# A third arm for experts of up to 64 rows, plain fp32 last half-pieces, and expert weights stored piece by piece

## The chip, the cores and the metric

The kernel runs on one core of one Trainium2 chip. The metric is the device time of one execution in microseconds. Before the change, three runs took 2416.90, 2423.72 and 2423.22 us (median 2423.22); the execution that the profiler recorded took 2418.95 us.

## The reference

One block of a diffusion transformer on 2048 rows of 1024 fp32 numbers. A first part (modulated RMS norm, a spatial gating unit, a bidirectional gated linear attention, an output projection) gives h; then comes a mixture of experts with a two-level router, and a final RMS norm:

```python
hn2 = modulate(rmsnorm(h, g_norm2), sh2, sc2)
# router: the best of 8 groups, then the best 2 of its 8 experts; gate = p_top * softmax(l_top)
# for each expert e, on the rows that chose it:
hblk = silu(xblk @ w1[e]) * (xblk @ w3[e])     # 1024 -> 512
yb   = (hblk @ w2[e]) * gate                   # 512 -> 1024, summed back to the rows
h = h + g2 * y
return rmsnorm(h, g_final)
```

There are 64 experts of three 512 x 1024 matrices (6 MB each in fp32) and 2048 x 2 = 4096 choices, 64 rows to an expert on average. With the reference's inputs, 41 experts get 64 rows or fewer, 16 get 65 to 128, and 7 get 129 to 220; the first of these 7 is number 8, the last number 39, and from number 40 on 21 of 24 have 64 or fewer.

## The kernel before

The first part (lines 111 to 842) and the router (lines 845 to 1150) come first. The change touches the expert stage, lines 1153 to 1390.

*Weights.* An expert has 12 pieces of 128 partitions x 1024 columns (512 KB): 8 for w1 and w3 side by side ("up"), 4 for w2 ("down"). `seq` (line 596) orders them: up of e+1, then down of e. `wload` (line 604) puts one DMA per piece on SyncE's queue, into the oldest of NR = 28 buffers. In DRAM, w_e is laid out by expert, partition, piece, so each partition's 4 KB of a piece lie 48 KB from the next partition's.

*fp32 in three passes.* Both operands of a product are split in a high part rounded to fp32r (ScalarE, a copy) and the remainder (VectorE, a subtraction), and TensorE runs high x high, high x low and low x high: three fp32r matmuls instead of one in plain fp32. `split_w` (line 79) does it for a half-piece of 512 columns, into a ring of R = 8 pairs wh and wl (line 1227); `need` (line 1232) keeps the splits LA = 4 half-pieces ahead of the matmuls in program order. The rows' side is split by `xprep` (line 1192: TensorE transposes the gathered rows, ScalarE and VectorE split them into xhe and xle) and by `hsplit` (line 1205, into hhe and hle).

*Order.* The schedule is written by hand: each engine executes its instructions in program order. One turn of the loop over e (line 1372) does `up(e + 1)`, counts and loads, then `down(e)`. Inside `block` (line 1256) a table `at` hangs other work on half-piece numbers: `hsplit` at half-piece 4 of up; `xprep` of the expert after next at half-piece 4 of down; the transposes of the GLU's result at half-piece 6. `glu` (line 1210) is a Silu on ScalarE and a product on VectorE, `yevac` (line 1214) scales the down result on VectorE, `scat` adds it to the output rows by an indirect DMA on GpSimd's queue.

*Arms.* How many rows an expert has is known on the device only. `count` (line 1277) reads nblk, the number of blocks of 128 rows, into a register of every engine, and up and down each have two arms under `tc.If`: `two` (above 128 rows; each split half-piece serves two blocks) and `one`. `both` (line 1239) emits the two with the same ring positions. `more` (line 1268) gathers the second block's rows, and `rest` (line 1290) handles blocks beyond the second.

Of the kernel before, what the change touches and what calls it, by code (L numbers as in the profile page):

```python
# [23 lines left out]
G, NE, EG, F = 8, 64, 8, 512  # L24
KF = F // P
# [5 lines left out]
def kernel(ctx: ExitStack, tc: tile.TileContext, a: dict, out: bass.AP):  # L31
    nc = tc.nc
    vec, act, pool, pe, sp = nc.vector, nc.scalar, nc.gpsimd, nc.tensor, nc.sync

    ctx.enter_context(tc.manual_schedule())
    const = ctx.enter_context(tc.tile_pool(name="const", bufs=1))
# [75 lines left out]
    wk = es.enter_context(tc.tile_pool(name="p1a", bufs=1))  # L112
# [112 lines left out]
    KG, PV, KZ, VV, LA, PB, PR, KDt, KE = ({} for _ in range(9))  # L225
# [182 lines left out]
    for half in range(2):  # L408
        for j in range(2):
            pm[j] = pt("mm", [P, 512], "pm")  # L410
        for k in range(KD):
            for j in range(2):
                pe.matmul(pm[j][0:2], sig[:, k], mtile[half * KD + k][:, j * 512:(j + 1) * 512],
                          start=k == 0, stop=k == KD - 1)
# [184 lines left out]
            seq += [(e + 1, k) for k in range(KD)]  # L599
        seq += [(e, KD + k) for k in range(KF)]  # L600
    W, WT = {}, []
    NW, NR = 25, 28

    def wload(n, eng=sp):

        for m in range(len(W), min(n, len(seq))):
            if m < NR:
                WT.append((wa if m < 14 else wb if m < NW else wk).tile([P, D], F32, name=f"we{m}", tag="w" if m < NW else f"we{m}"))
            e, k = seq[m]
            W[e, k] = WT[m % NR]  # L610
            eng.dma_start(out=W[e, k], in_=a["w_e"][e, :, k * D:(k + 1) * D])

    es = ExitStack()
    wk = es.enter_context(tc.tile_pool(name="p1c", bufs=1))
# [173 lines left out]
    for it in range(NT):  # L788
        ti = T - it
        n = ti - 1  # L790
# [59 lines left out]
    wk = es.enter_context(tc.tile_pool(name="p1d", bufs=1))  # L850
# [302 lines left out]
    nblk = const.tile([1, NE], I32, name="nblk")  # L1153
# [20 lines left out]
    four = lambda t: t.rearrange("p (c n) -> p c n", c=4)  # L1174
# [2 lines left out]
    ci_ = wk.tile([1, NE], I32, name="ci_")  # L1177
    vec.tensor_scalar(ci_, pc[0:1], float(P - 1), None, op0=OP.add)
    vec.tensor_scalar(nblk, ci_, 7, None, op0=OP.logical_shift_right)
    most = wk.tile([1, 1], I32, name="most")  # L1180
    vec.tensor_reduce(most, nblk, axis=mybir.AxisListType.X, op=OP.max)
    BOUND = "a count of at most S rows over blocks of P"

    xhl = [wk.tile([P, KD, P], F32R, name=n) for n in ("xhe", "xle")]
    hx = [wk.tile([P, KF, P], F32R, name=n) for n in ("hhe", "hle")]
    hx2 = [wk.tile([P, KF, P], F32R, name=n) for n in ("hh2", "hl2")]
    sh = wk.tile([P, F], F32, name="she")
    sh2 = [wk.tile([P, F], F32, name=f"sh2{i}") for i in range(2)]
    y1 = wk.tile([P, D], F32, name="y1")
# [2 lines left out]
    def xprep(x, hl, tp):  # L1192
        xh, xl = hl
        for c in range(KD):
            pe.transpose(four(tp[c // 4])[:, c % 4], x[:, c * P:(c + 1) * P], ident)  # L1195
        for q in range(2):
            qs = slice(4 * q, 4 * q + 4)
            act.activation(xh[:, qs], four(tp[q]), AF.Copy)
            vec.tensor_tensor(xl[:, qs], four(tp[q]), xh[:, qs].bitcast(F32), op=OP.subtract)

    def htr(sh, th):
        for i in range(KF):
# [2 lines left out]
    def hsplit(th, hx):  # L1205
        hh, hl = hx
        act.activation(hh, four(th), AF.Copy)
        vec.tensor_tensor(hl, four(th), hh.bitcast(F32), op=OP.subtract)

    def glu(pa, sh):  # L1210
# [18 lines left out]
    hpos = {v: p for p, v in enumerate(hseq)}  # L1229
    nsp = 0  # L1230

    def need(p):
        nonlocal nsp
        while nsp <= min(p, len(hseq) - 1):
            e, k, i = hseq[nsp]
            split_w(W[e, k][:, i * 512:(i + 1) * 512], *ring[nsp % R])
            nsp += 1

    def both(two, one):

        nonlocal nsp
        n0 = nsp
        two()
        n1, nsp = nsp, n0
        yield
        one()
        assert nsp == n1

    def mms(o, hl, k, i, nk, ring_):
        mm3(o, hl[0][:, k], hl[1][:, k], *ring_, k == 0, k == nk - 1)  # L1250
# [2 lines left out]

        return [t.rearrange("p (k n) -> p k n", k=KD) for t in (xgr[e % 3], xqr[e % 2])]

    def block(base, n, outs, hls, at):

        for q in range(n + (LAG if len(outs) > 1 else 0)):
            if q < n:
                need(base + q + LA)  # L1260
                if q in at:
                    at[q]()
            for j, (o, hl) in enumerate(zip(outs, hls)):
                p = q - j * LAG
                if 0 <= p < n:
                    mms(o[p % 2], hl, p // 2, p % 2, n // 2, ring[(base + p) % R])

    def more(e):

        n = nc.values_load(nblk[0:1, e:e + 1], engines=[mybir.EngineType.Pool], min_val=0, max_val=S // P,  # L1270
                           skip_runtime_bounds_check_because=BOUND)
        with tc.If(n > 1, preferred_fallthrough_block=False):
            gath(xq[e % 2], col(idx, NE + e))

    NB_ = {}

    def count(e):
        return nc.values_load(nblk[0:1, e:e + 1], min_val=0, max_val=S // P, skip_runtime_bounds_check_because=BOUND)

    def again(e, ks, outs, hl):  # L1280

        wh, wl = ring[nsp % R]
        raw = y2[:, F:]
        for k in range(ks[0], ks[1]):
            for i in range(2):
                pool.dma_start(out=raw, in_=a["w_e"][e, :, k * D + i * 512:k * D + (i + 1) * 512])
                split_w(raw, wh, wl)
                mms(outs[i], hl, k - ks[0], i, ks[1] - ks[0], (wh, wl))

    def rest():  # L1290

        x, hl = xq[0], rows2(0)
        n = nc.values_load(most, min_val=0, max_val=S // P, skip_runtime_bounds_check_because=BOUND)
        with tc.If(n > 2, preferred_fallthrough_block=False):
            for e in range(NE):
                n = count(e)
                with tc.If(n > 2, preferred_fallthrough_block=False):
                    with tc.For_i(2, n, 1) as i:
                        tb2 = wk.tile([P, 2], F32, name="tb2")
                        pool.dma_start(out=tb2, in_=tabD[bass.ds(i * P + e * S, P)])  # L1300
                        ix2 = wk.tile([P, 1], I32, name="ix2")
                        pool.tensor_copy(ix2, tb2[:, 0:1])
                        gath(x, ix2)
                        xprep(x, hl, TP)
                        again(e, (0, KD), PA, hl)
                        glu(PA, y2[:, 0:F])
                        htr(y2[:, 0:F], TH[1])
                        hsplit(TH[1], hx2)
                        again(e, (KD, KD + KF), PA, hx2)
                        yevac(PA, tb2[:, 1:2], y2)  # L1310
                        scat(y2, ix2)

    def up(e):

        at = {4: lambda: hsplit(TH[0], hx)} if e else {}
        base = hpos[e, 0, 0]

        def two():
            xprep(xq[e % 2], rows2(e), PY)
            block(base, 2 * KD, (PA, TP), (xhl, rows2(e)), at)  # L1320
            glu(PA, sh)
            glu(TP, sh2[e % 2])

        def one():
            block(base, 2 * KD, (PA,), (xhl,), at)
            glu(PA, sh)

        g = both(two, one)
        with tc.If(NB_[e] > 1, preferred_fallthrough_block=False) as f:
            next(g)  # L1330
        with f.Else():
            next(g, None)

    def down(e):

        base = hpos[e, KD, 0]
        at = {}
        if e + 2 < NE:
            at[4] = lambda: xprep(xg[(e + 2) % 3], xhl, TP)
        if e + 1 < NE:  # L1340
            at[6] = lambda: htr(sh, TH[0])

        def two():
            htr(sh2[e % 2], TH[1])
            hsplit(TH[1], hx2)
            block(base, 2 * KF, (PY, PA), (hx, hx2), at)
            yevac(PA, col(gate, NE + e), y2)
            scat(y2, col(idx, NE + e))

        def one():  # L1350
            block(base, 2 * KF, (PY,), (hx,), at)

        g = both(two, one)
        with tc.If(NB_[e] > 1, preferred_fallthrough_block=False) as f:
            next(g)
        with f.Else():
            next(g, None)
        yevac(PY, col(gate, e), Y[e % 2])
        scat(Y[e % 2], col(idx, e))

# [52 lines left out]
def _layout(inp):  # L1413
# [26 lines left out]
    z["b_r72"] = np.concatenate([A["b_router_g"], A["b_router_e"]], axis=1)  # L1440
    w13 = np.concatenate([A["w1"][0].reshape(NE, KD, P, F), A["w3"][0].reshape(NE, KD, P, F)], axis=3)
    w2 = A["w2"][0].reshape(NE, KF, P, D)
    z["w_e"] = np.concatenate([w13, w2], axis=1).transpose(0, 2, 1, 3).reshape(NE, P, 12 * D)
    z["g_final"] = A["g_final"].reshape(1, D)
    j, i = np.meshgrid(np.arange(P), np.arange(P), indexing="ij")
    same = j // CB == i // CB
# [27 lines left out]
```

## Time and profile before

| | |
|---|---|
| median of three runs | 2423.22 us |
| profiled execution | 2418.95 us, its span 2417.3 us |
| mean granted TensorE clock | 0.969 of full |
| TensorE busy | 2279.6 us (94%), 11932 matmuls |
| VectorE busy | 1929.6 us (80%) |
| ScalarE busy | 1438.4 us (60%) |
| GpSimd busy | 727.9 us (30%) |
| DMA | 613.42 MB, mean 254 GB/s |
| weight splits (line 80, line 81) | 1536 each, from 1038.3 to 2356.3 us |

Busy times are unions over the span, so the shares mix stages. The expert stage fills the second half, from 1038 to 2356 us. A matmul's record lasts longer than the distance to the next one, since matmuls are pipelined; what one costs is read from start to start. The same holds, less strongly, on VectorE and ScalarE. "issue" is a wait for nothing that the profile shows.

### The profile page before, as it was taken

The numbers are of one execution on the slowest core, as the hardware profiler recorded it, in microseconds if no ns is written. First come the engines' busy times: TensorE is split into PE (matmuls) and PEld (weight loads), VectorE is DVE, ScalarE is ACT, GpSimd is POOL, SyncE is SP. The second block draws the span as 40 slices with busy tenths as digits, with TensorE's granted clock in tenths as the row PEclk, the third lists the DMA queues.
The fourth block names the chain that finished last, engine by engine and source line by source line (L and its number), as shares of the span: only waits on it lengthen the run. The fifth ranks groups of instructions, "written<-read, shape, count | busy, mean of one in ns | idle before, by whom it ended". The sixth has DMA issues, their size and how long they took to land.

```text
span 2417.3 us, 40083 instructions
## 1 busy us (share of the span) xinstructions
PE 2279.6 (94%) x11932; PEld 1879.8 (78%) x11932; DVE 1929.6 (80%) x4302; ACT 1438.4 (60%) x2731; POOL 727.9 (30%) x602
## 2 busy tenths in 40 slices
PE   8999999999999899889999999999999999999980
PEld 3888888978777788778777888888777788888870
DVE  4555566567786788789887899999686699999986
ACT  3544443433323222378776788888575588888873
POOL 1123311147673122237521122323131232322220
PEclk9899999999999999989999999999999999999995
DMA  7333332256664654589998899999996799999947
GB/s 273 110 102 100 106 108 97 97 179 213 221 221 155 233 209 177 184 309 377 332 305 263 285 379 371 367 353 347 328 322 192 219 360 371 369 357 357 364 144 295
DMA packets 193220, 613.42 MB, mean 254 GB/s; under 512 B 36557, under 2 KB 36685, under 8 KB 192854
## 3 DMA queue, kind: packets, MB, share of 16 engines
q1 hardware_dynamic: 152358, 516.56, 58.8%
q0 software_dynamic: 38048, 87.95, 12.3%
q10 hardware_dynamic: 2448, 4.46, 0.5%
q8 instruction: 178, 2.92, 0.5%
q14 instruction: 188, 1.54, 0.2%
HBM read 547.42 MB, written 102.28 MB: 269 GB/s over the span
## 4 chain that ended last, share of the span: by engine, by line
PE 33%; DVE 12%; DMA 7%; issue 5%; ACT 0%; DVEq 0%; another core or an unknown queue 0%; SPq 0%; POOLq 0%; ACTq 0%; POOL 0%
DVE wl L81 9%; PE pa L84 6%; PE pa L86 6%; PE pa L85 6%; DMA we<-in_w_e_dram 4%; PE py L86 3%; PE py L84 3%; PE py L85 3%; DMA accD<-y,idx 2%; PE tpe L1195 1%; DVE y L1217 1%; PE tpe L85 1%; PE tpe L84 1%; PE tpe L86 1%; DMA hf<-accD 1%
## 5 line engine op out<-in xcount | busy, mean ns | idle before, releaser
L81 DVE TENSOR_TENSOR wl<-we,wh 128x512 fp32r<-128x512 f32 x1536 | 954.2, 682 | 83.6 <-ACT wh L80 77.0
L80 ACT ACTIVATE wh<-we 128x512 fp32r<-128x512 f32 x1536 | 892.4, 630 | 146.9 <-DVE wl L81 46.4
L84 PE MATMUL pa<-wh,xhe 128*128 128x512 f32 x1024 | 403.4, 394 | 9.5 <-ACT wh L80 6.3
L86 PE MATMUL pa<-wh,xle 128*128 128x512 f32 x1024 | 399.9, 391 | 0.0
L85 PE MATMUL pa<-wl,xhe 128*128 128x512 f32 x1024 | 399.5, 390 | 0.0
L1220 POOL DMA_INDIRECT accD<-y,idx x71 | 238.8, 3364 | 530.7 <-DVE y L1217 446.7
L84 PEld LDWEIGHTS pa<-wh,xhe 128*128 128x128 f32 x1024 | 192.3, 188 | 69.9 <-issue 28.5
L86 PEld LDWEIGHTS pa<-wh,xle 128*128 128x128 f32 x1024 | 192.3, 188 | 40.7
L85 PEld LDWEIGHTS pa<-wl,xhe 128*128 128x128 f32 x1024 | 192.5, 188 | 37.6
L84 PE MATMUL py<-wh,hhe 128*128 128x512 f32 x512 | 213.7, 417 | 6.9 <-ACT wh L80 6.4
L1162 POOL DMA_INDIRECT xg<-hnD,idx x64 | 93.5, 1461 | 417.2 <-DVE wl L81 143.2
L86 PE MATMUL py<-wh,hle 128*128 128x512 f32 x512 | 202.9, 396 | 1.6 <-issue 1.3
L85 PE MATMUL py<-wl,hhe 128*128 128x512 f32 x512 | 201.3, 393 | 3.2 <-DVE wl L81 3.2
L86 PEld LDWEIGHTS py<-wh,hle 128*128 128x128 f32 x512 | 97.3, 190 | 25.7 <-issue 3.4
L349 POOL TENSOR_SCALAR sc<-sc,dec 64x128 f32<-64x128 f32 x140 | 111.4, 795 | 19.1 <-PE po L682 7.8
L84 PEld LDWEIGHTS py<-wh,hhe 128*128 128x128 f32 x512 | 97.5, 190 | 24.8 <-issue 6.3
L85 PEld LDWEIGHTS py<-wl,hhe 128*128 128x128 f32 x512 | 97.8, 191 | 16.0 <-issue 0.2
L1070 POOL DMA_INDIRECT tabD<-pair,ri x32 | 70.0, 2187 | 91.3 <-DMA tabD<-pair,ri 58.8
L86 PE MATMUL pmx<-hi,mld 128*128 128x512 f32 x224 | 89.6, 400 | 5.6 <-DVE mld L81 5.6
L1217 DVE SCALAR_TENSOR_TENSOR y<-py,gate,g2b 128x512 f32<-128x512 f32 x128 | 89.7, 740 | 4.1 <-PE py L86 4.1
L84 PE MATMUL pmx<-hi,mhd 128*128 128x512 f32 x224 | 91.4, 408 | 0.4 <-ACT mhd L80 0.4
L85 PE MATMUL pmx<-lo,mhd 128*128 128x512 f32 x224 | 88.6, 396 | 0.0
(417 smaller groups left out, 4660.1 us busy)
## 6 DMA issues: line engine op xcount, KB each, us to landing
we<-in_w_e_dram SPq DMA_DIRECT2D x765, 512.0 KB
wt<-in_w_modB_dram SPq DMA_DIRECT2D x32, 512.0 KB
kve<-kveD SPq DMA_DIRECT2D x48, 256.0 KB
wt<-in_w_modA_dram SPq DMA_DIRECT2D x16, 512.0 KB
x<-in_x_dram SPq DMA_DIRECT2D x16, 512.0 KB
xD<-xf POOLq DMA_DIRECT2D x32, 256.0 KB
mfd<-mxD SPq DMA_DIRECT2D x16, 512.0 KB
xd<-in_x_dram SPq DMA_DIRECT2D x16, 512.0 KB
```

Source lines behind the costliest of these rows:

```text
L80: act.activation(hi, raw, AF.Copy)
L81: vec.tensor_tensor(lo, raw, hi.bitcast(F32), op=OP.subtract)
L84: pe.matmul(o, lh, wh, start=start, stop=False)
L85: pe.matmul(o, lh, wl, start=False, stop=False)
L86: pe.matmul(o, ll, wh, start=False, stop=stop)
L349: pool.tensor_scalar(s1[64:128, hs], s0[64:128, hs], dec[64:128, ci, h:h + 1], None, op0=OP.mult)
L1070: pool.indirect_dma_start(out=tabD, out_offset=bass.IndirectOffsetOnAxis(ap=ri[:, i:i + 1], axis=0), in_=pair[:, i], in_offset=None)
L1162: pool.indirect_dma_start(out=x, out_offset=None, in_=hnD, in_offset=bass.IndirectOffsetOnAxis(ap=ix, axis=0), bounds_check=S - 1, oob_is_ ...
L1195: pe.transpose(four(tp[c // 4])[:, c % 4], x[:, c * P:(c + 1) * P], ident)
L1217: vec.scalar_tensor_tensor(y[:, c], py[i], gt, g2b[:, c], op0=OP.mult, op1=OP.mult)
L1220: pool.indirect_dma_start(out=accD, out_offset=bass.IndirectOffsetOnAxis(ap=ix, axis=0), in_=y, in_offset=None, bounds_check=S - 1, oob_is ...
```

## The change

- `nhalf`, the number of half-blocks of 64 rows, stands beside nblk; `count` and `more` read it, and `arms` replaces `both` with three arms: `two` (nhalf above 2), `one` (2) and `few` (up to 1).
- The high part of the input lies in the last 128 columns of a wider tile xx, and `xprep` copies the low part's first 64 rows in front of it, on ScalarE, for every expert. The first 128 columns of xx are then low rows 0 to 63 and high rows 0 to 63.
- The few arm of up (`block2`) runs each weight half-piece against these in two matmuls, with wh and with wl; output partitions 0 to 63 hold the low rows' product, 64 to 127 the high rows'. `glu2` adds the two halves before Silu and product.
- `hsplit` also keeps the last two of the four hidden slices in plain fp32 (hf). The last half-pieces of down, 2 in `one` and 4 in `few`, are not split: TensorE multiplies hf by the weight piece itself in plain fp32.
- NR is 27 instead of 28. w_e lies in DRAM by expert, piece, partition: each piece is one stretch of 512 KB.

```diff
-    NW, NR = 25, 28
+    NW, NR = 25, 27
...
-            eng.dma_start(out=W[e, k], in_=a["w_e"][e, :, k * D:(k + 1) * D])
+            eng.dma_start(out=W[e, k], in_=a["w_e"][e, k])
...
+    vec.tensor_scalar(ch_, pc[0:1], float(P // 2 - 1), None, op0=OP.add)
+    vec.tensor_scalar(nhalf, ch_, 6, None, op0=OP.logical_shift_right)
...
-    xhl = [wk.tile([P, KD, P], F32R, name=n) for n in ("xhe", "xle")]
+    LO, HI = slice(0, P // 2), slice(P // 2, P)
+    xx = wk.tile([P, KD, P // 2 + P], F32R, name="xhe")
+    xhl = [xx[:, :, P // 2:], wk.tile([P, KD, P], F32R, name="xle")]
...
+    hf = wk.tile([P, 2, P], F32, name="hfe")
...  (xprep)
+        if hl is xhl:
+            act.activation(xx[:, :, LO], xl[:, :, LO].bitcast(F32), AF.Copy)
...  (hsplit)
+        if th is TH[0]:
+            act.activation(hf, four(th)[:, 2:4], AF.Copy)
...  (need, with raw)
-            split_w(W[e, k][:, i * 512:(i + 1) * 512], *ring[nsp % R])
+            if nsp not in raw:
+                split_w(W[e, k][:, i * 512:(i + 1) * 512], *ring[nsp % R])
...  (arms)
+        with tc.If(NB_[e] > 1, preferred_fallthrough_block=False) as f:
+            with tc.If(NB_[e] > 2, preferred_fallthrough_block=False) as g:
+                arm(two)
+            with g.Else():
+                arm(one)
+        with f.Else():
+            arm(few)
...  (block, with raw)
+                if n - raw <= p < n:
+                    e, k, i = hseq[base + p]
+                    pe.matmul(o[i], hf[:, p // 2 - 2], W[e, k][:, i * 512:(i + 1) * 512], start=False, stop=p // 2 == n // 2 - 1)
...
+    def block2(base, n, at):
+        for q in range(n):
+            need(base + q + LA)
+            if q in at:
+                at[q]()
+            for j, w in enumerate(ring[(base + q) % R]):
+                pe.matmul(PA[q % 2], xx[:, q // 2, 0:P], w, start=q < 2 and j == 0, stop=q // 2 == n // 2 - 1 and j == 1)
+
+    def glu2(t):
+        act.activation(t[HI], PA[0][HI], AF.Copy)
+        act.activation(sh[HI], PA[1][HI], AF.Copy)
+        vec.tensor_tensor(sh[LO], PA[0][LO], t[HI], op=OP.add)
+        vec.tensor_tensor(t[LO], PA[1][LO], sh[HI], op=OP.add)
+        act.activation(sh[LO], sh[LO], AF.Silu)
+        vec.tensor_tensor(sh[LO], sh[LO], t[LO], op=OP.mult)
...  (up)
+        def few():
+            block2(base, 2 * KD, at)
+            glu2(sh2[e % 2])
...  (down)
         def one():
-            block(base, 2 * KF, (PY,), (hx,), at)
+            block(base, 2 * KF, (PY,), (hx,), at, 2)
+        def few():
+            block(base, 2 * KF, (PY,), (hx,), at, 4)
...  (_layout)
-    z["w_e"] = np.concatenate([w13, w2], axis=1).transpose(0, 2, 1, 3).reshape(NE, P, 12 * D)
+    z["w_e"] = np.concatenate([w13, w2], axis=1)
```

## Rows read from the trace of the kernel before

**Rows 1.** Windows: length, busy us (count) of PE, PEld, DVE, ACT, POOL, PEclk, DMA, GB/s.
```profile
10.00:35.00 25.00, 25.00 (x62) 4.99 (x60) 7.46 (x20) 5.77 (x8) 1.96 (x7) 1.00 1.03 409
1050.00:1070.00 20.00, 19.81 (x96) 16.14 (x95) 18.45 (x31) 17.11 (x30) 2.07 (x2) 1.00 1.03 408
1450.00:1600.00 150.00, 148.39 (x698) 121.20 (x698) 150.00 (x248) 130.60 (x232) 44.14 (x17) 1.00 1.00 366
```

**Rows 2.** Waits, 1100 to 2350 us: us in total, times, longest us.
```profile
PEld pa L84 <- issue: 27.6, 46, 0.7
...
ACT wh L80 <- issue: 13.6, 4, 6.4
...
ACT wh L80 <- DMA we<-in_w_e_dram: 4.3, 7, 0.7
```

**Rows 3.** VectorE's groups, 1966.3 to 2111.9 us: busy us, mean ns | idle before.
```profile
L81 DVE TENSOR_TENSOR wl<-we,wh 128x512 fp32r<-128x512 f32 x192 | 117.9, 674 | 0.0
L1217 DVE SCALAR_TENSOR_TENSOR y<-py,gate,g2b 128x512 f32<-128x512 f32 x18 | 12.5, 732 | 0.0
L1199 DVE TENSOR_TENSOR xle<-tpe,xhe 128x512 fp32r<-128x512 f32 x16 | 10.2, 671 | 0.0
...
L1212 DVE TENSOR_TENSOR she<-she,pa 128x512 f32<-128x512 f32 x8 | 5.4, 669 | 0.0
```

**Rows 4.** Timeline of VectorE, 2013 to 2032 us: start, length, merged instructions.
```profile
2013.52 0.67 DVE L1212 TENSOR_TENSOR she<-she,pa 128x512 f32<-128x512 f32 x1
2014.12 3.08 DVE L81 TENSOR_TENSOR wl<-we,wh 128x512 fp32r<-128x512 f32 x5
2017.13 1.27 DVE L1199 TENSOR_TENSOR xle<-tpe,xhe 128x512 fp32r<-128x512 f32 x2
2018.33 1.88 DVE L81 TENSOR_TENSOR wl<-we,wh 128x512 fp32r<-128x512 f32 x3
...
2031.69 0.67 DVE L1212 TENSOR_TENSOR she<-she,pa 128x512 f32<-128x512 f32 x1
```

**Rows 5.** Timeline of TensorE, 2009 to 2020 us.
```profile
2009.16 0.39 PE L84 MATMUL pa<-wh,xhe 128*128 128x512 f32 x1
...
2011.88 0.39 PE L84 MATMUL pa<-wh,xhe 128*128 128x512 f32 x1
...
2015.28 1.03 PE L1195 MATMUL tpe<-cst,xg 128*128 128x128 f32 x8
...
2016.07 0.47 PE L84 MATMUL py<-wh,hhe 128*128 128x512 f32 x1
...
2019.72 0.19 PEld L84 LDWEIGHTS pa<-wh,xhe 128*128 128x128 f32 x1 [0.63 <-issue]
```

**Rows 6.** Timeline of ScalarE, 2012 to 2019 us.
```profile
2012.08 0.60 ACT L1211 ACTIVATE she<-pa 128x512 f32<-128x512 f32 x1 [1.41 <-PE pa L86]
2012.79 2.73 ACT L80 ACTIVATE wh<-we 128x512 fp32r<-128x512 f32 x5
2015.91 1.08 ACT L1198 ACTIVATE xhe<-tpe 128x512 fp32r<-128x512 f32 x2 [0.40 <-PE tpe L1195]
2016.88 2.71 ACT L80 ACTIVATE wh<-we 128x512 fp32r<-128x512 f32 x5
```

**Rows 7.** Timeline in a two-block expert, 1194 to 1197 us.
```profile
1194.58 0.69 DVE L81 TENSOR_TENSOR wl<-we,wh 128x512 fp32r<-128x512 f32 x1 [0.64 <-ACT wh L80]
...
1195.30 0.64 ACT L80 ACTIVATE wh<-we 128x512 fp32r<-128x512 f32 x1 [0.75 <-DVE wl L81]
...
1195.96 0.69 DVE L81 TENSOR_TENSOR wl<-we,wh 128x512 fp32r<-128x512 f32 x1 [0.69 <-ACT wh L80]
```

**Rows 8.** ScalarE's groups, 1966.3 to 2111.9 us.
```profile
L1211 ACT ACTIVATE she<-pa 128x512 f32<-128x512 f32 x8 | 4.8, 598 | 11.2 <-PE pa L86 11.2
```

**Rows 9.** TensorE's groups, 10 to 34 us, plain fp32 matmuls.
```profile
L413 PE MATMUL pm<-wt,sig 128*2 128x512 f32 x57 | 24.6, 592 | 0.0
```

**Rows 10.** Groups over the whole span, the same line 413.
```profile
L413 PE MATMUL pm<-wt,sig 128*2 128x512 f32 x64 | 29.6, 626 | 5.3 <-DMA wt<-in_w_modA_dram 5.3
```

More of the change, by code (lines that the diff above doesn't have):

```diff
@@ L1179 @@
     vec.tensor_scalar(nblk, ci_, 7, None, op0=OP.logical_shift_right)
+    nhalf = const.tile([1, NE], I32, name="nhalf")
+    ch_ = wk.tile([1, NE], I32, name="ch_")
+    vec.tensor_scalar(ch_, pc[0:1], float(P // 2 - 1), None, op0=OP.add)
+    vec.tensor_scalar(nhalf, ch_, 6, None, op0=OP.logical_shift_right)
     most = wk.tile([1, 1], I32, name="most")
@@ L1230, with need @@
     nsp = 0
-    def need(p):
+    def need(p, raw=()):
         nonlocal nsp
@@ L1235, in need, with arms, arm @@
             e, k, i = hseq[nsp]
-            split_w(W[e, k][:, i * 512:(i + 1) * 512], *ring[nsp % R])
+            if nsp not in raw:
+                split_w(W[e, k][:, i * 512:(i + 1) * 512], *ring[nsp % R])
             nsp += 1
-    def both(two, one):
+    def arms(e, two, one, few):
         nonlocal nsp
[L1242 to L1247, printed above, removed]
+        n0, done = nsp, []
+        def arm(f):
+            nonlocal nsp
+            nsp = n0
+            f()
+            done.append(nsp)
+        with tc.If(NB_[e] > 1, preferred_fallthrough_block=False) as f:
[5 more added lines that the diff above has]
+            arm(few)
+        assert len(set(done)) == 1
     def mms(o, hl, k, i, nk, ring_):
@@ L1254, in rows2, with block @@
         return [t.rearrange("p (k n) -> p k n", k=KD) for t in (xgr[e % 3], xqr[e % 2])]
-    def block(base, n, outs, hls, at):
+    def block(base, n, outs, hls, at, raw=0):
+        raws = range(base + n - raw, base + n)
         for q in range(n + (LAG if len(outs) > 1 else 0)):
             if q < n:
-                need(base + q + LA)
+                need(base + q + LA, raws)
                 if q in at:
@@ L1264, in block, with count @@
                 p = q - j * LAG
-                if 0 <= p < n:
+                if n - raw <= p < n:
+                    e, k, i = hseq[base + p]
+                    pe.matmul(o[i], hf[:, p // 2 - 2], W[e, k][:, i * 512:(i + 1) * 512], start=False, stop=p // 2 == n // 2 - 1)
+                elif 0 <= p < n:
                     mms(o[p % 2], hl, p // 2, p % 2, n // 2, ring[(base + p) % R])
+    def block2(base, n, at):
[12 more added lines that the diff above has]
+        vec.tensor_tensor(sh[LO], sh[LO], t[LO], op=OP.mult)
     def more(e):
-        n = nc.values_load(nblk[0:1, e:e + 1], engines=[mybir.EngineType.Pool], min_val=0, max_val=S // P,
+        n = nc.values_load(nhalf[0:1, e:e + 1], engines=[mybir.EngineType.Pool], min_val=0, max_val=2 * S // P,
                            skip_runtime_bounds_check_because=BOUND)
-        with tc.If(n > 1, preferred_fallthrough_block=False):
+        with tc.If(n > 2, preferred_fallthrough_block=False):
             gath(xq[e % 2], col(idx, NE + e))
     NB_ = {}
-    def count(e):
-        return nc.values_load(nblk[0:1, e:e + 1], min_val=0, max_val=S // P, skip_runtime_bounds_check_because=BOUND)
+    def count(e, t=nhalf):
+        return nc.values_load(t[0:1, e:e + 1], min_val=0, max_val=(2 if t is nhalf else 1) * S // P, skip_runtime_bounds_check_because=BOUND)
     def again(e, ks, outs, hl):
@@ L1285, in again @@
             for i in range(2):
-                pool.dma_start(out=raw, in_=a["w_e"][e, :, k * D + i * 512:k * D + (i + 1) * 512])
+                pool.dma_start(out=raw, in_=a["w_e"][e, k, :, i * 512:(i + 1) * 512])
                 split_w(raw, wh, wl)
@@ L1295, in rest @@
             for e in range(NE):
-                n = count(e)
+                n = count(e, nblk)
                 with tc.If(n > 2, preferred_fallthrough_block=False):
@@ L1326, in one @@
             glu(PA, sh)
[L1328 to L1332, printed above, removed]
+        def few():
+            block2(base, 2 * KD, at)
+            glu2(sh2[e % 2])
+        arms(e, two, one, few)
     def down(e):
@@ L1350, in one @@
         def one():
-            block(base, 2 * KF, (PY,), (hx,), at)
[L1353 to L1357, printed above, removed]
+            block(base, 2 * KF, (PY,), (hx,), at, 2)
+        def few():
+            block(base, 2 * KF, (PY,), (hx,), at, 4)
+        arms(e, two, one, few)
         yevac(PY, col(gate, e), Y[e % 2])
```

## Prediction

> **What bounds the kernel now.** Read the busy times by stretch first [rows 1]. In the expert stage's long runs of one-block experts (1450 to 1600 us) VectorE is busy 150.00 of 150 us, TensorE 148.39, ScalarE 130.60, and DMA has a share of 1.00 at 366 GB/s. Three resources look full, so the second view is who waited for whom over the whole stage [rows 2]. ScalarE waited for a landing weight piece 4.3 us in all, 0.7 us at the longest: DMA is full because it refills buffers as fast as they are released, not because it is late. The third view, VectorE's groups over eight experts [rows 3], has idle 0.0 on every line. VectorE sets the pace there; from product to product one expert takes 2031.69 - 2013.52 = 18.17 us [rows 4]. TensorE follows closely: 12 matmuls in 2011.88 - 2009.16 = 2.72 us, or 0.227 each [rows 5]. Its 72 matmuls are 16.34 us, its 8 input transposes 0.79 (2015.28 to 2016.07), its 4 others 0.4 at the same rate, and the jump into the next arm costs 0.6 (0.63 on issue) [rows 5]: 18.1 us.
>
> The reference's routing on its inputs gives 41 experts of up to 64 rows, 16 of 65 to 128, and 7 above (none over 256); call them few, one and two.
>
> **VectorE's account, few.** A split subtraction costs 0.602 us: five lie between 2014.12 and 2017.13 [rows 4]. One expert has 24 of these, two input subtractions at 0.60, one subtraction for the hidden rows like these, one product (0.60) and two evictions at 0.66 (their 0.732 less the 0.07 by which neighbours overlap) [rows 3]: 24 x 0.602 + 4 x 0.60 + 2 x 0.66 = 18.17, as measured. A few expert drops four splits (its last four half-pieces go raw to TensorE) and gains two additions of half the partitions but the same 512 columns. I take 0.60 for each; bounds 0.5 and 0.67, the busy duration. Net: -2.41 + 1.20 = -1.21 us.
>
> **The new wait.** The copy of xle's first 64 rows into xhe's tile runs on ScalarE, behind both input copies and ahead of the next weight copy, and reads what VectorE writes last in the input preparation. Today ScalarE runs ahead: after its two input copies it starts the next weight copy at 2016.88 [rows 6], while VectorE begins the input subtractions only at 2017.13 [rows 4]. ScalarE works in program order, so from now on it stands until VectorE's second subtraction ends, at 2018.40 (2017.13 + 1.27), and the weight copies queue behind it. The hand-over is seen where the two engines alternate in a two-block expert [rows 7]: VectorE ends at 1194.58 + 0.69 = 1195.27 and ScalarE starts at 1195.30 (0.03); from ScalarE's start to VectorE's next is 1195.96 - 1195.30 = 0.66. ScalarE's copies start 0.53 apart when nothing holds them ((2.73 - 0.63)/4 [rows 6]). So: copy at 2018.43, weight copy at 2018.96, VectorE's next split at 2019.62, where it was 2018.33 [rows 4]. VectorE stands 1.29 us per expert, and its queue holds all later splits, for which TensorE waits. Bounds: 0.76 if the copy itself cost nothing (1.29 - 0.53), 1.39 if it took its whole 0.63 with no overlap. Nought is excluded by the order on ScalarE, unless VectorE is no longer last; that is the first rival.
>
> The split GLU adds a second ring of waits: two copies on ScalarE (TensorE has finished some 1.5 us before VectorE arrives, so these are hidden: the one Silu waits 1.41 us for TensorE today [rows 6] while VectorE is still four splits away), then addition, Silu, product. From the first addition's start: 0.67 busy, 0.03, Silu 0.60 [rows 8], 0.03: product at +1.33, against +1.20 by the two additions. The next weight copy starts 0.71 after the Silu (2012.79 - 2012.08 [rows 6]), at +1.41, and its split 0.66 later at +2.07, against +1.93. Stall 0.13 + 0.14 = 0.27; bounds 0 and 0.6.
>
> Few: 18.17 - 1.21 + 1.29 + 0.27 = 18.52, that is +0.35 us; 41 x 0.35 = 14 us lost. TensorE is no bound there: 16 matmuls fewer in the up block (-3.63); a plain fp32 matmul of 512 columns is two records of 0.429 (57 records in 24.6 us [rows 9]; 64 records for the 32 calls of line 413 [rows 10]), 0.858 against 3 x 0.227 = 0.681, four of them +0.71; 18.1 - 2.9 = 15.2 us. ScalarE trades four copies for two evictions, the xle copy and the small fp32 copy: no more work than before, only in worse order.
>
> In VectorE's rows a split lasts 0.674 and the next starts after 0.602, so neighbours overlap by 0.07 [rows 3, 4]. The Trainium skill (page "VectorE: DVE Perf Modes", section "Two Vector instructions with no wait between them") says an instruction whose input starts in another quadrant than the last one read from that memory is held until all earlier ones are done. By it the first addition, which reads partition 64 up, would lose these 0.07 us, 41 x 0.07 = 3 us more over the stage. No row of before has such a pair, and the sum goes without it.
>
> **One.** VectorE: -2 x 0.602 + 1.29 = +0.09. TensorE: two raw half-pieces +0.35, so 18.1 + 0.35 = 18.45. If the two don't add, an expert takes 18.45 (+0.28); if VectorE's stand starves TensorE in full, 18.45 + 1.29 (+1.57). I take +0.7, nearer the lower end, because the ring holds eight half-pieces: 16 x 0.7 = 11 us. **Two.** TensorE bounds; per half-piece VectorE idles 0.69 of 1.38 us (1194.58 to 1195.96) [rows 7], so a stand of 1.29 is made good within two half-pieces, costing TensorE between 0 and 1.29. I take 0.7: 7 x 0.7 = 5 us.
>
> **The other edits.** The DRAM layout: 512 KB pieces that already lie in one stretch (w_modA, 10 to 35 us) move at 409 GB/s at a DMA share of 1.03; w_e pieces with 4 KB rows 48 KB apart, with a backlog (1050 to 1070 us), at 408 and 1.03 [rows 1]. Same speed; and a faster landing could save at most the 4.3 us of [rows 2]. I take nought, bounds -4 and 0. One buffer fewer (27 for 28) costs one piece of lead, a sum that the same row hides: nought to 2. Two small VectorE operations for nhalf before the first count: under 0.5 us. The last expert is few: TensorE ends alone, 4 x 0.177 = 0.7.
>
> **Sum.** 14 + 11 + 5 + 1 = 31 us. The profiled execution took 2418.95 us (span 2417.3); 2450. The median of the three runs is 4.3 us above it, so 2454.
>
> **Rivals.** (1) *The wait costs nothing* (faster). VectorE would no longer be last, say because TensorE's raw half-pieces, 3.4 us without a split, give it time to catch up. Then few is 18.17 - 1.21 + 0.27 = 17.23 (-0.94): -38; one +0.28: +4; two 0; 1: -33 us, 2390. For it: VectorE gets 3.4 us of TensorE time for free. Against it: few leaves TensorE 15.2 us and VectorE 17 us of work, so VectorE can't be off the path. It decides where the stand is below about 0.7 us: 41 x (0.94 - 0.7) = 10 us, what one and the ends cost. Chance 0.17. (2) *About half the stand is paid*: within 0.3% (7 us, about what a measurement can tell), 2423. Chance 0.11. (3) *Code fetch* (slower still). Each arm's jump now passes two other arms. Today a jump costs TensorE 27.6 us over 46 times, 0.6 each, and ScalarE waited 13.6 us on issue in 4 places, 3.4 each, 6.4 the longest [rows 2]. If one expert in four paid 3.4 us on ScalarE or VectorE, which have no slack, 16 x 3.4 = 54 us come on top: 2508. Against it: 57 one-block experts pass a two-block arm today with VectorE idle 0.0. Chance 0.08. The Trainium skill (page "Runtime: NRT & Kernel Launch", section "Instruction fetch mechanics") says a taken branch whose target lies outside the fetched pages stalls until the page has come, which would be this rival; today's trace agrees for those few places only. (4) *The layout does not do what it says*: as costed, it moves nothing; that is in the forecast.
>
> **Numbers.** Forecast 0.64 (2454; its own range 2436 to 2480), rivals 0.17, 0.11, 0.08. By the bounds: few from -1.41 + 0.76 = -0.65 (additions at 0.5, no GLU stall) to -1.07 + 1.39 + 0.6 = +0.92; one +0.28 to +1.57; two 0 to 1.29; with the ends -25 to +75 us, 2398 to 2498, if all fell on one side. Range 2412 to 2484: it cuts these corners and leaves out rival 3 and most of rival 1. Faster 0.19, same 0.12, slower 0.69.
>
> **What would show it.** VectorE idle in front of wl in few experts, once per expert about 1.3 us, released by ScalarE's wh, and ScalarE's xhe copy waiting for VectorE's xle; few experts 18.4 to 18.7 us apart; plain fp32 records of 0.43 us; waits for we landings unchanged. Wrong if few experts come 17.3 us apart, if VectorE idles nowhere, or if waits of several us on issue stand at the arms.

## The result and the profile after

The changed kernel takes 2605.66 us (median of 4 runs, 2589.7 to 2608.19) where the one before takes 2422.18 beside it: a ratio of 1.0748, 95% interval 1.0701 to 1.0794, 183 us slower. The forecast was 2454. The direction was right, and the size was short by a factor of six. The profiled execution took 2604.47 us.

Waits of the changed kernel over its expert stage, 1100 to 2540 us (us in total, times, longest), against [rows 2]:

```profile
DVE wl L81 <- ACT wh L80: 180.0, 185, 4.8
...
PEld py L84 <- issue: 93.5, 42, 7.0
...
ACT she L1310 <- DVE she L1308: 71.0, 36, 2.0
...
PE py L84 <- issue: 54.2, 10, 6.7
ACT xhe L1208 <- DVE xle L1206: 52.0, 59, 1.2
...
ACT wh L80 <- issue: 30.5, 12, 5.2
...
PE th L1212 <- issue: 16.5, 4, 6.9
DVE wl L81 <- DMA we<-in_w_e_dram: 16.0, 9, 4.6
...
ACT wh L80 <- DMA we<-in_w_e_dram: 8.9, 8, 4.6
```

Two things are new. The copy that the change adds (L1208) waits for VectorE 59 times, as forecast. And TensorE waits "on issue", which is for nothing that the profile shows, 10 times for 5 us in the mean at the first matmul of a down block (py) and 4 times in front of th; the row of before had 46 such waits at an arm, 0.7 us at the longest [rows 2]. But the kernel before had a long one too, in the same view:

```profile
PE th L1203 <- issue: 4.6, 1, 4.6
```

Waits for landings of we did not stay as they were: 24.9 us in all (8.9 on ScalarE, 16.0 on VectorE) against 4.3 on ScalarE alone. The four of 3.7 to 4.6 us begin inside gaps of TensorE like the one below; the others are 0.3 to 1.1 us, and in a_layout 11.5 us of such waits cost no time.

Windows of the changed kernel (length, busy us of PE, PEld, DVE, ACT, POOL, PEclk, DMA, GB/s), against the first and last of [rows 1]:

```profile
10.00:35.00 25.00, 25.00 (x72) 5.66 (x70) 8.32 (x21) 5.77 (x8) 1.94 (x7) 1.00 1.03 410
...
1450.00:1600.00 150.00, 134.02 (x482) 76.32 (x482) 126.95 (x205) 109.19 (x206) 33.63 (x14) 0.97 0.93 334
```

VectorE is busy 127 of 150 us where it was busy 150. Nothing is full any more; every engine waits at times.

From one eviction of py to the next, the experts now come (mean; before in brackets): few 21.26 us (18.70), one 24.69 (20.6), two 31.57 (29.9). Few experts fall into two kinds. An undisturbed one, VectorE's timeline (start, length, merged instructions, idle before):

```profile
2109.69 0.68 DVE L1308 TENSOR_TENSOR she<-pa,sh 64x512 f32<-64x512 f32 x1
2110.30 0.67 DVE L1309 TENSOR_TENSOR sh<-pa,she 64x512 f32<-64x512 f32 x1
2111.08 0.68 DVE L1311 TENSOR_TENSOR she<-she,sh 64x512 f32<-64x512 f32 x1
2112.17 0.69 DVE L81 TENSOR_TENSOR wl<-we,wh 128x512 fp32r<-128x512 f32 x1 [0.41 <-ACT wh L80]
2113.02 1.29 DVE L1206 TENSOR_TENSOR xle<-tpe,xhe 128x512 fp32r<-128x512 f32 x2 [0.15 <-ACT xhe L1205]
2115.52 1.90 DVE L81 TENSOR_TENSOR wl<-we,wh 128x512 fp32r<-128x512 f32 x3 [1.22 <-ACT wh L80]
...
2129.00 0.68 DVE L1308 TENSOR_TENSOR she<-pa,sh 64x512 f32<-64x512 f32 x1
```

It takes 2129.00 - 2109.69 = 19.31 us, where one before took 18.17 [rows 4]. The stand of 1.22 us is there, once per expert, as forecast at 1.29. ScalarE shows its cause; the copy of xle starts 0.03 us after VectorE's second subtraction ends, and the weight copies are queued behind it:

```profile
2112.39 1.08 ACT L1205 ACTIVATE xhe<-tpe 128x512 fp32r<-128x512 f32 x2 [0.61 <-PE tpe L1202]
2114.34 0.63 ACT L1208 ACTIVATE xhe<-xle 128x512 fp32r<-128x512 f32 x1 [0.87 <-DVE xle L1206]
2114.87 2.71 ACT L80 ACTIVATE wh<-we 128x512 fp32r<-128x512 f32 x5
```

In the later runs of few experts, about every second one is of the other kind, 23.7 to 26 us. TensorE between its up and its down block there:

```profile
2171.79 0.50 PE L1302 MATMUL pa<-wl,xhe 128*128 128x512 f32 x1
2177.64 0.76 PE L84 MATMUL py<-wh,hhe 128*128 128x512 f32 x1 [5.35 <-issue]
2178.21 0.63 PE L85 MATMUL py<-wl,hhe 128*128 128x512 f32 x1
2178.63 0.63 PE L86 MATMUL py<-wh,hle 128*128 128x512 f32 x1
```

For 5.35 us TensorE starts nothing. In this gap (2171.8 to 2177.7) the instruction queue q8 moved one block of 16 KB (queue, packets, MB, share):

```profile
q8 instruction: 1, 0.02, 1.4%
```

Its packet runs from 1.86 to 3.14 us after the gap's start, and the first matmul follows 2.2 us after its end. One block alone would prove little, since the queue moves 161 of them between 1058 and 2545 us, one per 9.2 us. But TensorE has 22 gaps above 2.5 us between 1060 and 2550 us, and a block is being moved in every one of them; so it is in the 3 such gaps of the kernel before.

After the gap the matmuls start 0.43 us apart where they started 0.23 apart [rows 5]: the granted clock has fallen from 1.00 to its lower level (0.74 in the mean over 2178.6 to 2185.2, part of it at 1.2 GHz). The wide spacing lasts until 2182.05, some 4 us.

### The profile page after: what moved, and what is told of

It is laid out like the page before. It is cut to its first block, busy times and chain, and to the rows that moved or that the text cites. A ratio compares the mean times of both kernels' runs of the same rounds, so it can differ in the third digit from the quotient of the medians.

```text
span 2602.5 us, 38388 instructions
## 1 busy us (share of the span) xinstructions
PE 2302.3 (88%) x11080; PEld 1702.3 (65%) x11080; DVE 1882.1 (72%) x4190; ACT 1396.4 (54%) x2745; POOL 617.2 (24%) x601
## 3 DMA queue, kind: packets, MB, share of 16 engines
q0 software_dynamic: 37904, 87.42, 11.5%
## 5 line engine op out<-in xcount | busy, mean ns | idle before, releaser
L81 DVE TENSOR_TENSOR wl<-we,wh 128x512 fp32r<-128x512 f32 x1340 | 837.7, 684 | 210.3 <-ACT wh L80 188.1
L80 ACT ACTIVATE wh<-we 128x512 fp32r<-128x512 f32 x1340 | 742.6, 624 | 171.2 <-DVE wl L81 39.8
L1231 POOL DMA_INDIRECT accD<-y,idx x71 | 141.6, 1994 | 749.4 <-DVE y L1228 681.8
L1302 PEld LDWEIGHTS pa<-wl,xhe 128*128 128x128 f32 x656 | 123.4, 188 | 177.2 <-DVE wl L81 167.5
L84 PE MATMUL py<-wh,hhe 128*128 128x512 f32 x316 | 145.6, 461 | 86.5 <-issue 54.2
L1291 PE MATMUL py<-we,hfe 128*128 128x512 f32 x392 | 184.3, 593 | 0.0
L1206 DVE TENSOR_TENSOR xle<-tpe,xhe 128x512 fp32r<-128x512 f32 x128 | 82.7, 685 | 87.2 <-ACT xhe L1205 85.5
L86 PE MATMUL pa<-wh,xle 128*128 128x512 f32 x368 | 145.7, 396 | 0.0
L1205 ACT ACTIVATE xhe<-tpe 128x512 fp32r<-128x512 f32 x128 | 69.8, 594 | 101.3 <-PE tpe L1202 96.8
L349 POOL TENSOR_SCALAR sc<-sc,dec 64x128 f32<-64x128 f32 x140 | 112.8, 806 | 20.6 <-PE po L682 9.3
L1291 PEld LDWEIGHTS py<-we,hfe 128*128 128x128 f32 x392 | 67.1, 190 | 47.5 <-issue 47.3
```

What stands on the lines that cost most here:

```text
L84: pe.matmul(o, lh, wh, start=start, stop=False)
L86: pe.matmul(o, ll, wh, start=False, stop=stop)
L349: pool.tensor_scalar(s1[64:128, hs], s0[64:128, hs], dec[64:128, ci, h:h + 1], None, op0=OP.mult)
L1231: pool.indirect_dma_start(out=accD, out_offset=bass.IndirectOffsetOnAxis(ap=ix, axis=0), in_=y, in_offset=None, bounds_check=S - 1, oob_is ...
L1291: pe.matmul(o[i], hf[:, p // 2 - 2], W[e, k][:, i * 512:(i + 1) * 512], start=False, stop=p // 2 == n // 2 - 1)
L1302: pe.matmul(PA[q % 2], xx[:, q // 2, 0:P], w, start=q < 2 and j == 0, stop=q // 2 == n // 2 - 1 and j == 1)
```

## Experiments

Each number is the ratio to the kernel before, run beside it on the same chip, with its interval; 1% is 24 us. Theory A: waits for code, because the jumps pass longer arms. Theory B: hand-overs between ScalarE and VectorE. C: the DRAM layout. D: plain fp32 matmuls.

**a_layout**: before, with the layout and 27 buffers.

```
-    eng.dma_start(out=W[e, k], in_=a["w_e"][e, :, k * D:(k + 1) * D])
+    eng.dma_start(out=W[e, k], in_=a["w_e"][e, k])
```

> Before with the DRAM layout of w_e alone (each piece in one stretch, 27 buffers for 28). Theory A (the longer jumps over skipped arms make TensorE and ScalarE wait for code) and theory B (the hand-overs between ScalarE and VectorE cost more than I summed): the layout moves nothing, 2422 us within 7. Theory C (the layout loads the memory unevenly and delays landings): above 2440 us, with longer waits for we.

0.9991 (0.9981 to 1.0). C is out.

**b_thirdarm**: before, with an arm more that is only jumped over.

```
 with tc.If(NB_[e] > 1) as f:
+    with tc.If(NB_[e] > 2) as g:
+        arm(one)
+    with g.Else():
         arm(two)
 with f.Else():
     arm(one)
```

> Before with a third arm that no expert takes (a copy of the one-block arm), so that the jumps pass as much TensorE code as in the changed kernel, and nothing else. Theory A: most of the 183 us, 2520 to 2590 us, with one-block experts partly at 24 to 26 us and waits on issue of 5 to 7 us at the arms. Theory B, C and D (plain fp32 matmuls are slower): 2422 us within 7.

1.0631 (1.0611 to 1.0652), 152 us. No instruction of the new arm ever runs, and the waits are those of the changed kernel, ScalarE's too (waits 1100 to 2350 us, then TensorE's timeline):

```profile
ACT wh L80 <- issue: 68.5, 22, 4.9
...
PE py L84 <- issue: 49.2, 10, 5.6
```

```profile
2363.43 0.39 PE L86 MATMUL pa<-wh,xle 128*128 128x512 f32 x1
2368.96 0.76 PE L84 MATMUL py<-wh,hhe 128*128 128x512 f32 x1 [5.14 <-issue]
```

Of ScalarE's 19 waits on issue above 1.5 us in this window, 13 begin inside a gap of TensorE, so there TensorE is the first to stand. Theory A holds, and D isn't needed for it: this kernel has no raw half-piece.

**c_fewtwo**: the changed kernel without the arm one; larger experts of one block take two.

```
-            with tc.If(NB_[e] > 2) as g:
-                arm(two)
-            with g.Else():
-                arm(one)
+            arm(two)
```

> The changed kernel with two arms, few and two: experts of 65 to 128 rows take the two-block arm. The 16 of them then cost about 30 us each, as the seven two-block experts before. Theory A: few experts all at 19.3 us, no wait on issue above 2 us at their arms: 41 x 19.3 + 23 x 30 = 1481 us from expert to expert, where before it was 1306: about 2597 us. Theory B (stalls come from the few arm's own work): few experts stay at 21.3 in the mean, 41 x 2 more: about 2680 us.

1.1464 (1.1445 to 1.1484). The total fits neither number, because I took the two-block experts' price from a mean; side by side they are 37.8 us, so 16 x (37.8 - 18.2) = 314 and 41 x 0.9 = 37 make 2769, as measured; the sum was made after the result. The mean of few experts is 21.81 us, close to theory B's 21.3, but only because nine of the 40 intervals between evictions hold the up block of a two-block expert (32.45 us each). The runs decide: there few experts come 18.8 to 19.1 us apart throughout, with no long wait of TensorE at py in 1100 to 2350 us (one of 5.5 us stands at th). The stalls belong to the third arm, not to few's own work.

**d_latecopy**: the changed kernel, copy of xle two half-pieces later on ScalarE.

```
-            act.activation(xx[:, :, LO], xl[:, :, LO]...)      # in xprep, at[4]
+            at[6] = lambda: (htr(sh, TH[0]), xlate() ...)      # xlate: the same copy
```

> The changed kernel with the copy of xle's first 64 rows issued two half-pieces later on ScalarE, behind two more weight copies. Theory B: VectorE's stand of 1.2 us in front of wl goes, undisturbed few experts come 18.1 us apart in place of 19.3, 41 x 1.2 = 49 us less: about 2557 us. Theory A as the whole of the loss: experts that stall at a jump do so all the same and the stand is only a part of the wait, 2580 to 2606 us.

1.0432 (1.0413 to 1.045), 2521 us: 76 us less than the changed kernel, where B had 49; undisturbed few experts come 18.2 us apart. B holds for the stand, beside A; why the total fell by more than B's 49 is not shown.

**h_uponly and i_downonly**: the third arm of b_thirdarm in one of the two blocks (`arms(e, two, one)` with the inner If only there).

> Before with the third arm that no expert takes in the up block alone (its jump then passes 208 + 96 TensorE instructions, the down block's still 104). All three arms together cost 152 us. Theory W (it is the reach of one jump, past what has been fetched): the up jump alone pays most of it, 2520 to 2570 us. Theory V (it is the volume skipped, wherever): two thirds (96 of 144 instructions more), about 2517 us. Theory P (the down jump is at fault, since the waits stand there): about 2420 us.

> Before with the third arm that no expert takes in the down block alone (its jump passes 104 + 48 TensorE instructions, less than the 208 that the up jump passes today). Theory W: no more than today, 2418 to 2440 us. Theory V: one third of 152 us, about 2468 us. Theory P: most of it, above 2500 us.

1.0468 (1.0448 to 1.0489) and 1.0049 (1.0028 to 1.007): 113 and 12 us. TensorE's waits at py, first with the arm in the up block only; in the down-only kernel the longest such waits are at other places (th here), and few:

```profile
PE py L84 <- issue: 54.0, 11, 6.3
```

```profile
PE th L1203 <- issue: 8.4, 2, 4.4
```

So the up jump, over 304 TensorE instructions, is the cause, although the time is lost at the down block's start, one jump later. Theory P falls, and V too (two thirds to one third was expected, ten to one came). The expectations count the down block's arms as 104 and 48 TensorE instructions; with the 12 transposes that `at` hangs in it they are 128 and 72. The jump of i_downonly then passes 200, still below 208, and V's shares are 57 and 43%. The third arm lengthens the other engines' jumps too; that TensorE's counts is read from its gaps, not from a run. Together the two arms cost 152, more than 113 + 12.

**e_split**: d_latecopy with the up block cut in two, each half with its own three arms.

```
+        for h in range(2):
+            lo, hi = h * KD, KD if h == 0 else 99
             ...  # two, one, few over half-pieces lo to hi
             arms(e, two, one, few)
```

> The changed kernel with the late copy (2521 us) and the up block cut in two, each half with its own choice among three arms, so that no jump passes more than about 160 TensorE instructions; the same work and as much code. Theory W: the waits on issue go, few experts stay near 18.2 us and one-block experts near 18.2: 41 x 1.6 + 16 x 4 = about 130 us less, 2390 to 2430 us. Theory V: no less than 2521 us. If the second choice itself is dear (0.4 us on VectorE each): 64 x 0.4 = 26 us on top of either.

1.0101 (1.0076 to 1.0127), 2440 us: 80 us less with the same work and as much code, 10 us above W's range. The longest jump is now the down block's, over some 195 TensorE instructions counted as above. The instruction queue q8 moves 164 blocks in 1060 to 2383 us, as many as in the changed kernel (161): it isn't their number that costs. The waits (1100 to 2350 us):

```profile
PE py L84 <- issue: 11.8, 6, 2.2
```

**f_down2**: d_latecopy with one down arm for all one-block experts (raw = 4).

> The changed kernel with the late copy (2521 us), and in the down block one arm for all experts of one block (four raw half-pieces), so that its jump passes the two-block arm alone. TensorE pays 0.35 more for each of the 16 experts of 65 to 128 rows, 6 us. Theory W: the up jump still reaches too far, 2500 to 2530 us. Theory V: a third of the stalls goes, about 2480 us. Theory P: nearly all of them go, 2400 to 2430 us.

1.0308 (1.0289 to 1.0327), 2491 us: between W's and V's numbers; the stalls at py stay (34.4 us, 7 times, 6.1 the longest). W is right in the main, but the shorter down jump is worth 30 us here, where its third arm alone cost 12 in i_downonly.

**m_splitonly**: the changed kernel with the up block cut in two, nothing else.

> The changed kernel with the up block cut in two and nothing else (ScalarE's copy of xle's first rows where the change puts it). It prices that stand with nearly no waits for code around it: against 2440 us with the late copy. My sum's 1.29 us (less 0.05 for the copy's new place) x 41 few experts and about 0.3 x 16 others: 2440 + 58 = 2498 us, few experts at 19.3 us. If the stand mostly overlapped the waits for code: 2450 to 2465 us, few experts below 18.8.

1.0335 (1.0317 to 1.0354), 2499.6 us; few experts at 19.3. The stand costs 1.0335 - 1.0101, 57 us, and the long jump 1.0748 - 1.0335, 100 us; taken out in the other order, 76 (d_latecopy) and 80 (e_split).

What is left in e_split is 24 us above before, where my terms without the stand gave 33 below. Some 8 us of the 24 lie ahead of the first eviction of py (at 1081.55 us, before at 1073.78); no run asks why. Its VectorE, one few expert:

```profile
2108.62 1.29 DVE L1209 TENSOR_TENSOR xle<-tpe,xhe 128x512 fp32r<-128x512 f32 x2 [0.20 <-ACT xhe L1208]
...
2125.89 0.69 DVE L81 TENSOR_TENSOR wl<-we,wh 128x512 fp32r<-128x512 f32 x1 [0.36 <-ACT wh L80]
2126.78 1.29 DVE L1209 TENSOR_TENSOR xle<-tpe,xhe 128x512 fp32r<-128x512 f32 x2 [0.20 <-ACT xhe L1208]
```

18.16 us, with 17.0 of work by the rates of [rows 3, 4]. The next runs ask what holds it there.

**k_early, j_down2, l_raw6**: on e_split, input transposes at half-piece 2 (`at[2]` for `at[4]`); then, on k_early, one down arm, or six raw half-pieces and a lead of two (`LA = R - LAG - 3`).

> The kernel with the late copy and the up block cut in two (2440 us), with the input transposes two half-pieces earlier in the down block, so that VectorE no longer waits for them (0.2 to 0.8 us in each few expert). If VectorE sets the pace: few experts at 17.3 to 17.8 us, 41 x 0.6 = 25 us less, 2415 us. If the transfers set it (DMA share 0.99 at 365 GB/s): few experts stay at 18.2 us, 2440 us.

> The same with one arm in the down block for all experts of one block (four raw half-pieces). Theory W (the reach of one jump past fetched code): the waits on issue that are left at the down block (14.6 us in 5 places in few experts, 3.6 in 2 others, and the lower clock behind them) go, TensorE pays 6 us in the 16 larger ones: 10 to 20 us below the kernel without it. If these waits come from elsewhere: 5 us above it.

> The same as the kernel with the earlier transposes, with six raw half-pieces for few experts in place of four, and splits two half-pieces ahead in place of four. VectorE drops 2 x 0.60 us, TensorE gains 2 x 0.18. If VectorE still sets the pace in few experts: 41 x 0.8 to 1.2 = 33 to 49 us below the kernel without it. If the transfers set it: the same. If the shorter lead starves TensorE in the others: 23 x 0.5 = 12 us or more above it.

1.0169 (1.0151 to 1.0188), 1.0151 (1.0116 to 1.0185), 1.0392 (1.0371 to 1.0414): all misses, each slower than e_split. In k_early VectorE's idle time moved to xle and to the evictions:

```profile
2132.99 1.29 DVE L1209 TENSOR_TENSOR xle<-tpe,xhe 128x512 fp32r<-128x512 f32 x2 [0.78 <-ACT xhe L1208]
...
2137.37 1.61 DVE L1231 SCALAR_TENSOR_TENSOR y<-py,gate,g2b 128x512 f32<-128x512 f32 x2 [0.49 <-PE py L1294]
```

In l_raw6 VectorE had two splits fewer and few experts took 19.7 us, longer than k_early's 19.1.

**n_order, p_order2, q_apart**: on e_split, two splits issued between the additions and the product; then one down arm; then the copies and subtractions of the input two half-pieces later.

```
         vec.tensor_tensor(t[LO], PA[1][LO], sh[HI], op=OP.add)
+        need(p)                     # block2 stops two splits short
```

> The kernel with the late copy and the up block cut in two (2440 us), with two of the splits that few experts make near the end of the up block issued between the two additions and the product, so that VectorE has 1.2 us of work while ScalarE makes the Silu. If the hand-overs set the pace of few experts: the idle of 0.36 us behind the product and part of the 0.2 to 0.8 us in front of xle go, few experts at 17.3 to 17.8 us, 41 x 0.4 to 0.9 = 16 to 37 us less, 2403 to 2424 us. If the transfers set it (DMA share 0.98 at 370 GB/s): few experts stay at 18.2 us, 2440 us. If the two later splits starve TensorE, as the earlier transposes did: 2455 us.

> The same with one arm in the down block for all experts of one block. The waits on issue at the down block that are left go (14.6 us in 5 places and 3.6 in 2), TensorE pays 6 us in the 16 larger experts: 5 to 15 us below the kernel without it. If it is as without the late splits, where it gave 2 us (2456 after 2458): the same.

> The kernel with the late splits and one down arm (2429 us), with the input preparation taken apart in the down block: the transposes where they are, the copies and VectorE's subtractions two half-pieces later, behind two more splits. VectorE's last idle time in few experts (0.85 us in front of xle, which waits for the transposes by way of ScalarE) would be filled. If the hand-overs set the pace: few experts at 17.4 to 17.8 us, 41 x 0.5 to 0.9 = 20 to 37 us less, 2392 to 2409 us, faster than before. If the transfers set it (DMA share 0.98): few experts stay at 18.3 us, 2429 us. If the wait only moves on, to TensorE's start of the next up block and the evictions behind it: 18.2 to 18.4 us as well, with idle time of VectorE in front of y.

1.0085 (1.007 to 1.01), 1.0047 (1.0031 to 1.0063), 1.0035 (1.0022 to 1.0049). Few experts stay at 18.3, 18.3 and 18.15 us; the wait behind the product went and 0.85 us in front of xle came, then 0.7 to 0.9 in front of y.

**r_halfload**: q_apart with half of the weights' transfers.

```
+            if k % 2:
+                W[e, k] = W[e, k - 1]
+                continue
```

> The kernel with the input preparation taken apart (2427 us, few experts 18.15 us apart), with every second 512 KB piece of the experts' weights not loaded: the piece before it is used twice, so half of w_e's bytes are left out and all else is issued as before. If the transfers hold few experts at 18.2 us: they come 17.0 to 17.4 us apart, 41 x 0.9 = 37 us less, 2390 us. If the hand-overs between TensorE, ScalarE and VectorE hold them: 18.1 to 18.2 us as before, 2415 to 2427 us, at a DMA share near one half.

2417.18 us, 1.0003 (0.9986 to 1.0019). The transfers aren't what holds few experts: with DMA at 0.63 and 195 GB/s they come 2123.19 - 2105.05 = 18.14 us apart (window, VectorE, TensorE):

```profile
2085.00:2158.00 73.00, 67.71 (x259) 41.63 (x258) 69.69 (x114) 60.88 (x113) 11.68 (x8) 1.00 0.63 195
```

```profile
2105.05 1.61 DVE L1238 SCALAR_TENSOR_TENSOR y<-py,gate,g2b 128x512 f32<-128x512 f32 x2 [0.66 <-PE py L1304]
2106.58 3.10 DVE L81 TENSOR_TENSOR wl<-we,wh 128x512 fp32r<-128x512 f32 x5
2109.58 0.69 DVE L1229 TENSOR_TENSOR hle<-th,hhe 128x512 fp32r<-128x512 f32 x1
2110.18 5.50 DVE L81 TENSOR_TENSOR wl<-we,wh 128x512 fp32r<-128x512 f32 x9
...
2123.19 1.61 DVE L1238 SCALAR_TENSOR_TENSOR y<-py,gate,g2b 128x512 f32<-128x512 f32 x2 [0.66 <-PE py L1304]
```

```profile
2114.54 0.49 PE L1315 MATMUL pa<-wl,xhe 128*128 128x512 f32 x1
2115.64 0.47 PE L84 MATMUL py<-wh,hhe 128*128 128x512 f32 x1 [0.61 <-ACT sh L1319]
...
2123.45 0.79 PE L1315 MATMUL pa<-wh,xhe 128*128 128x512 f32 x1
```

A loop closes here. From the eviction, VectorE makes the splits that the up block still lacks, one by one, until TensorE's last up matmul at 2114.54 (9.5 us); the hand-over takes 1.1; TensorE's down block goes from 2115.64 to the next eviction at 2123.19 (7.55). During the down block VectorE may run only four half-pieces ahead, and stands.

**s_lead**: p_order2 with a lead that grows to eight half-pieces.

```
-                need(base + q + LA, raws)
+                need(base + q + LA + (max(0, q - 3) if raw else 0), raws)
...
+            need(base + 2 * KF + LA + 3)     # in the two-block arm, behind its down block
```

> The kernel with the late splits and one down arm (2429 us, few experts 18.3 us apart), with VectorE's and ScalarE's splits running up to eight half-pieces ahead in place of four while TensorE works on the raw half-pieces (which leave their ring slots free). Theory L (few experts go in a loop: VectorE's splits from the evictions to the end of the up block, some 9.4 us, the hand-over, 1.1, and TensorE's down block, 7.6; VectorE can't use its idle time because it may not run further ahead): four splits of 0.60 move out of the loop, and VectorE's own work with its last waits, 17.2 to 17.5 us, sets the pace: 41 x 0.8 to 1.1 = 33 to 45 us less, 2384 to 2396 us, faster than before. If each wait only moves on as in the last two kernels: few experts at 18.1 to 18.3 us, 2420 to 2430 us. If the transfers cannot follow the earlier splits: waits for we in front of wh, and 2410 us or more.

1.0073 (1.0057 to 1.0089). The loop is confirmed, with the period just above the 17.2 to 17.5 expected: in runs, few experts come 2125.63 - 2108.07 = 17.56 us apart and VectorE has nearly no idle time left in them (busy 71.79 of 73 us from 2085 to 2158).

```profile
2108.07 0.68 DVE L1314 TENSOR_TENSOR she<-pa,sh 64x512 f32<-64x512 f32 x1
...
2112.72 1.29 DVE L1209 TENSOR_TENSOR xle<-tpe,xhe 128x512 fp32r<-128x512 f32 x2 [0.25 <-ACT xhe L1208]
...
2125.63 0.68 DVE L1314 TENSOR_TENSOR she<-pa,sh 64x512 f32<-64x512 f32 x1
```

The total expected from it did not come: an expert of one block next to a larger one takes 19.4 us, and neighbouring two-block experts 41.3 where they took 37.8. Against p_order2, few experts gained 10 us in all (18.58 us in the mean for 18.83), since those next to larger ones gave back over half of what the runs had gained; one lost 10 (21.36 for 20.73) and two 10 (29.84 for 28.41). The edit also brings splits forward in the two-block arm, and no run tells apart what that does. No version found beats the kernel before.

## Why the prediction was wrong

The 181 us (7.48% of 2418) come apart by the ratios: 100 for the long jump (changed kernel against m_splitonly), 57 for the stand (m_splitonly against e_split), 24 for the rest; the first two depend on the order. My sum had 0, 64 (31 less the -33 of rival 1) and -33.

- **The stand** was right: 1.22 us in VectorE's rows against 1.29, the place, the cause, and 57 us, or 76 with the stalls still there (d_latecopy), against 64.
- **Code fetch is the step that failed first.** I had it as rival 3, with a chance of 0.08 and 54 us on top. Its argument against, that 57 one-block experts pass a two-block arm today with VectorE idle 0.0, was true of the arm that was there (208 TensorE instructions) and says nothing of one half as long again (304). The price was wrong too: I took 3.4 us on ScalarE for every fourth expert, and TensorE stands 5 to 7 us in up to every second one, at a lower clock afterwards. The Trainium skill (page "Runtime: NRT & Kernel Launch", section "Instruction fetch mechanics") says that a taken branch to a block that isn't loaded yet waits for it to be fetched. The traces agree: a 16 KB block is being moved in each of the 22 gaps. How far a jump may reach is told by these runs only from outside: 208 instructions cost next to nothing, 304 cost 113 us in the up block alone. The sign was in the trace of before, in the one 4.6 us wait of TensorE on issue, which I passed over.
- **VectorE's account of few was wrong as a bound.** Its work, 17.0 us by the rates, is near what s_lead shows (71.79/73 of 17.56, 17.3 us busy), but I let an expert take the sum of VectorE's work and stalls, 17.23 without the stand. It takes 18.15 to 18.2, set by the loop through both engines. Without the stand and the long jump that is up to 41 x 0.95 = 39 us of the 57 by which this term failed. By the means it is 48: in e_split few experts take 18.95 us for 18.70 before, +10 us in place of -38, with some stalls left in them. The new few experts of 18.52 us were 19.31.
- **The split GLU**, 0.27 us, was 0.17 in front of the product and 0.49 behind it, from start to start (0.41 of that idle); in n_order this wait went and the period stayed, so it was no term of a sum at all.
- **One** was forecast at +0.7 us. In m_splitonly, where the long jump is gone, the mean is 22.33 against 20.6 before, +1.7; in e_split, without the stand, 21.04, +0.4. **Two** stayed within 0.1 there.
- **Layout and buffer**, nothing: right (a_layout). **Plain fp32**: right within 0.04 us per record. Sixty records of L1291 in 28.2 us, at a granted clock of 0.97, are 0.47 each, against 0.429 at full clock [rows 9]:

```profile
L1291 PE MATMUL py<-we,hfe 128*128 128x512 f32 x60 | 28.2, 593 | 0.0
```

- **The held addition**, which I weighed and left out: a split and the first addition start 0.71 us apart (2108.98 and 2109.69), two splits 0.602. By the Trainium skill (page "VectorE: DVE Perf Modes", section "Two Vector instructions with no wait between them") it loses the overlap of 0.07; the trace has 0.11, some 4 us in all. No run tells its cause apart.

Not settled: why the time of the long up jump is lost one jump later, why both new arms cost 152 us where each alone cost 113 and 12, and where between 208 and 304 instructions the loss begins.

## What to carry to other kernels

Count the instructions that each engine's jump skips before adding an arm to a branch: code that never runs cost 6% here, and cutting one long choice into two short ones gave 80 to 100 us of the 181 back. In a kernel whose engines alternate, look for the loop through them (evict, split, multiply, evict) and for what limits the lead; the sum of the busiest engine's work is only a lower bound. A copy that reads what another engine writes last belongs behind that engine's next work, not in front of one's own.

## What the runs showed of the hardware that was not expected

A never taken arm in the up block stalled TensorE 5 to 6 us at a time (54.0 us in 11 places) and brought its granted clock down behind the gap (0.64 in the mean over 2107.2 to 2112.0 us of h_uponly, behind a gap of 4.93 us; 1.00 again over 2112.0 to 2118.0). Half the weight traffic (195 GB/s for 357 in the same window of q_apart) left the period of few experts at 18.14 us, although DMA had shown a share of 0.96 to 1.00: a full share was no sign of a bound.
